# A feed-forward's gate and up products in one written order, their weights' low parts on VectorE, and the down weights loaded behind them without a wait

## The chip, the cores and the metric

One core of a Trainium2 chip runs the kernel. Its engines are TensorE (PE: matmuls), VectorE (DVE), ScalarE (ACT), GpSimd (POOL) and SyncE (SP), which issues all the DMAs. Each engine carries out its own instructions in the order in which they stand in its program and waits on semaphores for the others. The metric is the device time of one execution in microseconds (us); a run's median, lowest and highest are given. One execution was taken with a profiler; its span lies within its device time.

## The reference, cut to what matters

One layer of an encoder: 1024 positions, width 1024, in float32. A feed-forward, a mixer (two kinds of attention), and a second feed-forward, each between RMS norms and added to the input by half, whole, and half.

```python
def swiglu(x, w_gate, w_up, w_down):          # x 1024x1024, D_FF = 2816
    return (jax.nn.silu(x @ w_gate) * (x @ w_up)) @ w_down

f1 = swiglu(rms_norm(h, ffn1_pre_g), ffn1_w_gate, ffn1_w_up, ffn1_w_down)
h = h + 0.5 * rms_norm(f1, ffn1_post_g)
mix = hybrid_mixer(rms_norm(h, mix_pre_g), ...)
h = h + rms_norm(mix, mix_post_g)
f2 = swiglu(rms_norm(h, ffn2_pre_g), ffn2_w_gate, ffn2_w_up, ffn2_w_down)
h = h + 0.5 * rms_norm(f2, ffn2_post_g)
```

## The kernel before

*Precision.* A float32 operand is held as a high part, rounded to the matmul's type, and a low part, the rest. A product is three matmuls: high by high, high by low, low by high (`three`). To make the parts of a weight, ScalarE casts it to the high part (L521) and GpSimd subtracts that from the weight (L522); the helper is `split`.

*Fewer products.* `ffn` (L544) treats gate and up as 22 units (p, m): 11 pairs of 256 columns, p = 0 to 10, with m = 0 for gate and m = 1 for up. A unit is a 2x2 block product done with seven block products instead of eight (Strassen's scheme in Winograd's form). The seven left sides come from the raw weights: product 0, 1 and 3 are blocks of the raw tile; 4, 5, 6 and 2 are sums s1, s2, s3 and a second s2 made by VectorE (L593, L595, L597, L601). L601 overwrites the first s2, so it waits until the low part of product 5, which GpSimd makes from it, is done (`read2`). The right sides are seven combinations of X, made once (`X.ready`). A product is 12 matmuls of 512 columns (4 blocks of depth, three matmuls each, L641).

*PSUM.* Products 0 and 1 add up in one bank (tile b), 5 has a bank of its own, products 6 and 3 share one half of a pair of banks (tile s), 4 and 2 the other half. ScalarE copies product 0 (L667) to uu. VectorE then adds: uu + product 5 (L724), that + product 6 (L730), and from these the four blocks of the result: block 3 (L756), 2 (L768), 1 (L773). Product 3 writes on into the bank that L730 reads, so it has to wait for L730; product 2 waits for L756. Multiplications by the sigmoid (L686, L701) make the hidden values. For each pair VectorE and ScalarE then form seven combinations of the hidden values (L819 to L826) and their high and low parts (L795, L798); SyncE stores them to DRAM (hs_d, L799). The last pair is stored plain (hp_d).

*Down.* Pairs 0 to 9 make five groups of two pairs (g = 0 to 4), the last pair stands by itself. A group is again seven products; weights are loaded as rawd (four per group, L868), summed by VectorE (td, L887 to L897), split by ScalarE (wdb, L521) and GpSimd (L522); hidden pieces are loaded back as ha (L910); 168 matmuls a group (L1045); VectorE adds the results up (L994, L1084).

*What sets the order.* `Plan` (L126) is a small event-driven planner that runs while the program is built. Each piece of work is a Python generator; it yields events and tokens it waits for, and then work of an engine with a planned price (L262 to L278) and a rank. Whenever a planned engine is free, the waiting piece of the best rank is written into its program. The order that comes out is fixed; on the chip each engine follows it. Rooms for raw tiles and weight tiles are tokens (`raw_tok`, `w_tok`). In `gate_up` a unit is two processes, `head` (products 0 and 1) and `body` (5, 6, 4, 3, 2), so units may interleave as the planner's prices have it. `down_loads` begins only when the next to last pair is stored:

```python
        def down_loads():
            yield stored[NP - 2]
```

## Time and profile before

| | us |
|---|---|
| median of 3 runs | 2594.76 |
| lowest to highest | 2591.78 to 2595.79 |
| the profiled execution, device time | 2596.65 |
| its span | 2594.2 |
| TensorE busy | 2339.3 (90%) |
| VectorE busy | 1538.4 (59%) |
| GpSimd busy | 1225.7 (47%) |
| ScalarE busy | 1037.8 (40%) |

The profiled execution is 2.45 us longer than its span, and 1.9 us above the median. The mean granted clock of TensorE was 0.951 of full speed. The stretches of the span: the input's norm and the first combinations of X until about 56 us, gate and up of the first feed-forward until 511.9, the way into its down part until 550.2, that part until about 743, the mixer until about 1851, the second feed-forward's combinations until 1888.1, its gate and up until 2337.1, the way into down until 2370.0, and down and the last norm until the end. Matmuls are pipelined: a matmul's own duration (about 0.39 us) is longer than the distance to the next.

### The profile page before, as it was taken

How to read it: one execution, taken by the hardware profiler on the slowest of the kernel's cores; microseconds unless marked ns; L12 is line 12 of the kernel's file. 1: busy time of each engine (PE TensorE's matmuls, PEld its weight loads, DVE VectorE, ACT ScalarE, POOL GpSimd, SP SyncE). 2: the span in 40 equal slices, each digit the busy share in tenths (PEclk: the TensorE clock that was granted, in tenths of full speed). 3: DMA queues.
4: the chain of work that ended last, by engine and by line, in shares of the span. 5: the costliest groups of instructions: out<-in, count | busy, mean ns of one | idle time of the engine just before them, and what ended most of it. 6: DMA issues, size and time to landing. Idle time of an engine off the chain costs nothing. (4 is left out here: it accounts for less than half of the span.)

```text
span 2594.2 us, 31044 instructions
## 1 busy us (share of the span) xinstructions
PE 2339.3 (90%) x11096; PEld 1942.6 (75%) x11096; DVE 1538.4 (59%) x2359; ACT 1037.8 (40%) x1958; POOL 1225.7 (47%) x900
## 2 busy tenths in 40 slices
PE   6999999879988995999998998998799999997997
PEld 4777777658868984888887777876577777785885
DVE  8765667446574101676667677247856766564656
ACT  5333333231124232666655555444433333334111
POOL 4444455254466351665543223556345544535445
PEclk8999999989999997999999998998899999998998
DMA  4233344477633133212222222665324434357762
GB/s 140 104 129 139 110 163 158 162 278 253 231 100 122 40 102 107 57 53 84 81 65 81 86 86 78 231 211 195 138 70 152 160 118 151 113 215 274 258 234 97
DMA packets 198010, 364.86 MB, mean 141 GB/s; under 512 B 40608, under 2 KB 112800, under 8 KB 197344
## 3 DMA queue, kind: packets, MB, share of 16 engines
q1 hardware_dynamic: 197856, 362.89, 41.0%
q8 instruction: 87, 1.43, 0.2%
q14 instruction: 67, 0.55, 0.1%
HBM read 240.02 MB, written 122.81 MB: 140 GB/s over the span
## 5 line engine op out<-in xcount | busy, mean ns | idle before, releaser
L641 PE MATMUL s<-xh,wt 128*128 128x512 f32 x1408 | 468.6, 401 | 49.7 <-DVE uu L730 42.4
L522 POOL TENSOR_TENSOR wt<-s,wt 128x512 fp32r<-128x512 f32 x176 | 248.9, 1426 | 286.7 <-ACT wt L521 276.7
L641 PEld LDWEIGHTS s<-xh,wt 128*128 128x128 f32 x1408 | 271.5, 193 | 120.2 <-issue 52.0
L641 PE MATMUL b<-xh,wt 128*128 128x512 f32 x1056 | 344.4, 394 | 0.0
L522 POOL TENSOR_TENSOR wt<-raw,wt 128x512 fp32r<-128x512 f32 x132 | 197.4, 1505 | 201.1 <-ACT wt L521 130.3
L641 PE MATMUL s<-xl,wt 128*128 128x512 f32 x704 | 280.6, 399 | 0.0
L1045 PE MATMUL b<-wdb,ha 128*128 128x512 f32 x864 | 207.5, 396 | 35.1 <-ACT wdb L521 32.7
L641 PEld LDWEIGHTS b<-xh,wt 128*128 128x128 f32 x1056 | 201.5, 191 | 42.7 <-ACT xh L430 0.2
L1045 PEld LDWEIGHTS b<-wdb,ha 128*128 128x128 f32 x864 | 165.1, 192 | 72.2 <-ACT wdb L521 34.0
L641 PE MATMUL b<-xl,wt 128*128 128x512 f32 x528 | 207.4, 393 | 0.0
L1045 PE MATMUL s<-wdb,ha 128*128 128x512 f32 x816 | 194.2, 394 | 5.6 <-POOL wdb L522 3.6
L1045 PEld LDWEIGHTS s<-wdb,ha 128*128 128x128 f32 x816 | 155.0, 190 | 39.5 <-POOL wdb L522 4.4
L1870 POOL TENSOR_TENSOR p<-p,rd 128x1024 f32<-128x1024 f32 x64 | 120.7, 1894 | 101.1 <-DVE rd L1867 92.6
L1410 PE MATMUL b<-xh,wh 128*128 128x512 f32 x384 | 163.8, 427 | 0.0
L641 PEld LDWEIGHTS s<-xl,wt 128*128 128x128 f32 x704 | 135.9, 193 | 27.9
L1410 PE MATMUL b<-xl,wh 128*128 128x512 f32 x384 | 155.0, 404 | 0.0
L1410 PE MATMUL b<-xh,wl 128*128 128x512 f32 x384 | 154.2, 401 | 0.0
L522 POOL TENSOR_TENSOR wdb<-rawd,wdb 128x1024 fp32r<-128x1024 f32 x34 | 81.9, 2409 | 142.8 <-ACT wdb L521 139.7
L522 POOL TENSOR_TENSOR wdb<-td,wdb 128x1024 fp32r<-128x1024 f32 x40 | 100.1, 2503 | 92.9 <-ACT wdb L521 87.4
L522 POOL TENSOR_TENSOR wl<-raw,wh 128x512 fp32r<-128x512 f32 (+3 forms) x88 | 110.3, 1273 | 61.7 <-ACT wh L521 46.6
L601 DVE TENSOR_TENSOR s<-raw,s 128x512 f32<-128x512 f32 x44 | 72.9, 1658 | 101.3 <-POOL wt L522 101.3
L283 PE MATMUL s<-qkT,qkT 96*128 96x512 f32 x384 | 104.5, 406 | 21.9 <-ACT p L1860 21.9
(290 smaller groups left out, 5171.1 us busy)
## 6 DMA issues: line engine op xcount, KB each, us to landing
hs_d<-hl SPq DMA_DIRECT2D x140, 512.0 KB
ha<-hs_d SPq DMA_DIRECT2D x70, 1024.0 KB
raw<-in_ffn_w_gate_dram SPq DMA_DIRECT2D x44, 512.0 KB
raw<-in_ffn_w_up_dram SPq DMA_DIRECT2D x44, 512.0 KB
rawd<-in_ffn_w_down_dram SPq DMA_DIRECT2D x44, 512.0 KB
raw<-in_w_in_dram SPq DMA_DIRECT2D x28, 512.0 KB
h<-res SPq DMA_DIRECT2D x16, 512.0 KB
lg_d<-lg SPq DMA_DIRECT2D x32, 256.0 KB
```

The source lines that it names most:

```text
L283: T.matmul(o, l, r, start=(i == 0), stop=(i == n - 1))
L522: yield pool(n, lambda: G.tensor_sub(lo, src, hi))
L601: yield dve(512, lambda: V.tensor_sub(s2, L(0, 1), s2))
L641: T.matmul(out(), l, r, start=(first and k == 0 and n == 0), stop=(k == 3 and n == 2), skip_group_check=True,)
L1045: T.matmul(ps, l, r, start=(fresh and n == 0), stop=(n == 5), skip_group_check=True)
L1410: T.matmul(bs.ps, l, r, start=(part == 0 and n == 0), stop=(part == 7 and n == 2))
L1870: yield pool(S, lambda: G.tensor_tensor(bx.p, bx.p, bx.rd.broadcast_to([P, S]), op=ALU.mult))
```

## The change

The products of gate and up are written in one sequence `seq`: in the round of unit u come its product 0, then products 3 and 2 of the unit before, then its products 1, 5, 6 and 4. One process steps through it (`step`), in the place of `head` and `body`. The weights' parts follow the same sequence; the high part stays on ScalarE (L648), the low part is VectorE's (L649), where it was GpSimd's. A raw tile's two halves are waited for and freed each for itself. The processes that load and prepare the weights go on to the down weights with no wait for a store, and the down weights' rooms are the same tokens. A pair's token `gate_tok` is given back without a wait for its store. At the start of the second feed-forward three raw tiles may be loaded instead of two. The planner's price of a VectorE instruction rises by 0.05 us. The sums of a unit are now L615, L619, L622 and L626 (L593, L595, L597, L601 before), the PSUM additions L760, L771, L780, L793, L800 (L724, L730, L756, L768, L773), the products L675 (L641), the stores L829, the loads of down weights L900, of hidden pieces L942, the down sums L919, L922, L924, L929 (L887, L890, L892, L897), the additions of down L1028 (L994).

```diff
-        return ("dve", 0.1 + n * 0.00105, fn)
+        return ("dve", 0.15 + n * 0.00105, fn)
...
-        raw_tok, w_tok, hl_tok = Tokens(4 if room is None else 2), Tokens(6 if room is None else 2), Tokens(3)
+        raw_tok, w_tok, hl_tok = Tokens(4 if room is None else 3), Tokens(6 if room is None else 2), Tokens(3)
 
         def more():
             yield room
-            plan.release(raw_tok, 2)
+            plan.release(raw_tok, 1)
             plan.release(w_tok, 4)
 
         if room is not None:
             spawn(more(), 7)
         gate_tok = Tokens(2)
         units = [(p, m) for p in range(NP) for m in range(2)]
-        raws = {u: ([], Event(2)) for u in units}
+
+
+        seq = [(units[0], 0), (units[1], 0), (units[0], 1), (units[1], 1)]
+        for n, u in enumerate(units):
+            if n > 1:
+                seq.append((u, 0))
+            if n:
+                seq += [(units[n - 1], 3), (units[n - 1], 2)]
+            if n > 1:
+                seq.append((u, 1))
+            seq += [(u, 5), (u, 6), (u, 4)]
+        seq += [(units[-1], 3), (units[-1], 2)]
...
+            yield from down_loads()
...
+            def one(u, i):
+                bx, wx = sums[u], ws[*u, i]
+                ev = raws[u][1]
+                yield {0: ev[0], 1: ev[1], 2: bx.made[3], 3: ev[1], 4: bx.made[0], 5: bx.made[1], 6: bx.made[2]}[i]
+                L = bx.L
+                src = {
+                    0: lambda: L(0, 0), 1: lambda: L(0, 1), 2: lambda: bx.s2, 3: lambda: L(1, 1),
+                    4: lambda: bx.s1, 5: lambda: bx.s2, 6: lambda: bx.s3,
+                }[i]()
+                w = wx[0].w = slot([P, 2, 4, P], F32R, "wt")
+                yield act(512, lambda: A.copy(w[:, 0], src))
+                yield dve(512, lambda: V.tensor_sub(w[:, 1], src, w[:, 0]))
                 if i == 5:
-                    plan.set(read2)
-                plan.set(ev)
-                plan.set(used)
-
-            def free():
-                yield used
-                plan.release(raw_tok, 2)
-
-            spawn(combos(), 7)
-            spawn(free(), 7)
-            for i, src, after in (
-                (0, L(0, 0), None), (1, L(0, 1), None), (5, s2, made[1]), (6, s3, made[2]),
-                (4, s1, made[0]), (3, L(1, 1), None), (2, s2, made[3]),
-            ):
+                    plan.set(bx.read2)
+                if i in (0, 1, 3):
+                    plan.set(bx.used[0 if i == 0 else 1])
+                plan.set(wx[1])
...
+            for u, i in seq:
+                if u not in sums:
+                    begin(u)
+                if i == 1:
+                    spawn(sums[u].combos(), 7)
                 yield w_tok
-                ws[p, m, i][0].w = slot([P, 2, 4, P], F32R, "wt")
-                spawn(one(i, src, after), 7)
-
-        def prep():
-            for p, m in units:
-                yield from prep_unit(p, m)
+                spawn(one(u, i), 7)
+            yield from down_prep()
...
+        def step(u, i, ub):
...
+            elif i == 6:
+                yield S2
+                yield from product(u, 6, s_bank(0), True)
+
+                def second():
+                    yield ub.added[0]
+                    yield dve(512, lambda: V.tensor_add(u3(), ub.s[:, 0, :], u2()))
+                    plan.set(ub.added[1])
+
+                spawn(second(), 3)
...
+            elif i == 3:
+                yield ub.added[1]
+                yield from product(u, 3, s_bank(0), False)
...
+            else:
+                yield ub.read[3]
+                yield from product(u, 2, s_bank(1), False)
...
         def gate_up():
-            for u in units:
-                yield unit_tok
-                if u[1] == 0:
-                    yield gate_tok
-                ub = Box()
-                ub.m1 = Event()
-                spawn(head(u, ub), 8)
-                spawn(body(u, ub), 8)
-                if u[1] == 1:
-                    spawn(pair_done(u[0]), 5)
+            ubs = {}
+            for u, i in seq:
+                if u not in ubs:
+                    yield unit_tok
+                    if u[1] == 0:
+                        yield gate_tok
+                    ub = ubs[u] = Box()
+                    ub.m1 = Event()
+                    ub.added = [Event(), Event()]
+                    ub.read = [None, Event(), Event(), Event()]
+                    if u[1] == 1:
+                        spawn(pair_done(u[0]), 5)
+                yield from step(u, i, ubs[u])
+            plan.release(raw_tok, 2)
...
-            yield stored[p]
             plan.release(gate_tok)
...
-        rd_tok, t_tok = Tokens(6), Tokens(1)
+        rd_tok, t_tok = raw_tok, Tokens(1)
...
         def down_loads():
-            yield stored[NP - 2]
...
         def down_prep():
+            for _ in range(3):
+                yield w_tok
...
-        spawn(down_loads(), 8)
-        spawn(down_prep(), 8)
```

VectorE in the middle of the first gate and up, before, from the sum that waits for GpSimd (s is a weight sum or the PSUM tile, uu and c a unit's results, hs the hidden sums):

```order
L601 TENSOR_TENSOR s_267_1691<-raw_1604,s_267_1691 128x512 [waits Pool_49]
L730 TENSOR_TENSOR uu_1657<-s_1701,uu_1657 128x512 [waits PE_49]
L773 TENSOR_TENSOR uu_1518<-s_1572,uu_1518 128x512 [waits PE_49]
L701 TENSOR_TENSOR uu_1381<-uu_1518,uu_1381 128x512 [waits DVE_49]
L819 TENSOR_TENSOR hs_1755<-uu_1381 128x512 [waits DVE_49]
L821 TENSOR_TENSOR hs_277_1756<-sg_1450,uu_1381 128x512
L820 TENSOR_TENSOR hs_1755<-hs_1755,sg_1450 128x512 [waits DVE_49]
L756 TENSOR_TENSOR uu_1657<-s_1701,uu_1657 128x512 [waits PE_49]
```

After, VectorE from the addition of product 5 to that of product 6 (wt is a weight's high and low part, hl a hidden sum's):

```order
L760 TENSOR_TENSOR uu_1946<-b_2000,uu_1946 128x512 [waits DMAHW2_49,PE_49]
L615 TENSOR_TENSOR s_315_2014<-raw_1806,raw_1869 128x512 [waits DMAHW3_49]
L649 TENSOR_TENSOR wt_2013<-s_294_1865,wt_2013 128x512 [waits Activation_49]
L828 TENSOR_TENSOR hl_2046<-hs_1991,hl_2046 128x512 [waits Activation_49]
L828 TENSOR_TENSOR hl_2062<-hs_1991,hl_2062 128x512 [waits Activation_49]
L649 TENSOR_TENSOR wt_2039<-raw_1869,wt_2039 128x512 [waits DMAHW5_49]
L828 TENSOR_TENSOR hl_2081<-hs_309_1992,hl_2081 128x512 [waits Activation_49]
L619 TENSOR_TENSOR s_315_2014<-s_315_2014,raw_1806 128x512 [waits DVE_49]
L622 TENSOR_TENSOR s_316_2015<-raw_1806 128x512
L771 TENSOR_TENSOR uu_1946<-s_2026,uu_1946 128x512 [waits PE_49]
```

L626 waits for VectorE itself (it is not within these rows), and between the two additions stand eight others, two of them low parts of weights.

SyncE at the end of the first gate and up, before (hp_d are the last pair's stores, rawd the down weights, ha the hidden pieces):

```order
L799 DMA hp_d<-hl_3706 256x1x512 [waits DMAHW1_49,DVE_49]
L910 DMA ha_3716<-hs_d 128x2x1024 [waits DMAHW2_49,PE_49]
L799 DMA hp_d<-hl_3713 256x1x512 [waits DMAHW3_49,DVE_49]
L910 DMA ha_3719<-hs_d 128x2x1024 [waits DMAHW4_49,PE_49]
L868 DMA rawd_3721<-in_ffn_w_down_dram 128x2x512 [waits DMAHW5_49]
L868 DMA rawd_3723<-in_ffn_w_down_dram 128x2x512 [waits DMAHW6_49,Pool_49]
L868 DMA rawd_3728<-in_ffn_w_down_dram 128x2x512 [waits DMAHW7_49]
L868 DMA rawd_3754<-in_ffn_w_down_dram 128x2x512 [waits DMAHW0_49,Pool_49]
```

After, from the last raw weights of gate and up:

```order
L517 DMA raw_3349<-in_ffn_w_up_dram 128x4x256 [waits DMAHW2_49,PE_49]
L900 DMA rawd_3372<-in_ffn_w_down_dram 128x2x512 [waits DMAHW3_49]
L829 DMA hs_d<-hl_3463 128x1024 [waits DVE_49]
L900 DMA rawd_3468<-in_ffn_w_down_dram 128x2x512 [waits DMAHW5_49,PE_49]
L829 DMA hs_d<-hl_3466 128x1024 [waits DMAHW6_49,DVE_49]
```

The first two of the four loads of down weights now stand right behind the last raw weights, among the stores of the last but one pair (hs_d); the other two follow six rows further down, and the last pair's stores (hp_d) begin six rows behind those.

VectorE at the same place, before, from the last unit's results to the down weights' sums (td):

```order
L701 TENSOR_TENSOR uu_3421<-uu_3561,uu_3421 128x512 [waits DVE_49]
L768 TENSOR_TENSOR c_540_3680<-s_3614,uu_3561 128x512 [waits PE_49]
L701 TENSOR_TENSOR sg_3478<-c_540_3680,sg_3478 128x512 [waits DVE_49]
L773 TENSOR_TENSOR uu_3561<-s_3614,uu_3561 128x512
L701 TENSOR_TENSOR uu_3421<-uu_3561,uu_3421 128x512 [waits DVE_49,Activation_49]
L798 TENSOR_TENSOR hl_3703<-uu_3421,hl_3703 128x512 [waits Activation_49]
L798 TENSOR_TENSOR hl_3706<-sg_3478,hl_3706 128x512 [waits Activation_49]
L798 TENSOR_TENSOR hl_3713<-uu_3421,hl_3713 128x512 [waits DMAHW4_49,Activation_49]
L887 TENSOR_TENSOR td_3757<-rawd_3723,rawd_3721 128x1024 [waits DMAHW7_49,DMAHW6_49,DMAHW5_49]
L890 TENSOR_TENSOR td_3758<-rawd_3728,td_3757 128x1024 [waits DMAHW7_49,DMAHW0_49,DVE_49]
L892 TENSOR_TENSOR td_3759<-rawd_3728,rawd_3723 128x1024
L897 TENSOR_TENSOR td_3758<-rawd_3754,td_3758 128x1024 [waits DMAHW0_49,Pool_49]
```

After:

```order
L919 TENSOR_TENSOR td_3667<-rawd_3468,rawd_3372 128x1024 [waits DMAHW5_49,DMAHW3_49]
L800 TENSOR_TENSOR uu_3422<-s_3496,uu_3422 128x512 [waits DVE_49]
L697 TENSOR_TENSOR sg_3489<-b_3537,sg_3489 128x512 [waits PE_49]
L922 TENSOR_TENSOR td_3668<-rawd_3580,td_3667 128x1024 [waits DMAHW4_49,DMAHW2_49,DVE_49]
L924 TENSOR_TENSOR td_3669<-rawd_3580,rawd_3468 128x1024
L760 TENSOR_TENSOR uu_3572<-b_3627,uu_3572 128x512 [waits PE_49]
L929 TENSOR_TENSOR td_3668<-rawd_3625,td_3668 128x1024 [waits DMAHW5_49,Pool_49]
L771 TENSOR_TENSOR uu_3572<-s_3641,uu_3572 128x512 [waits DVE_49,PE_49]
L780 TENSOR_TENSOR uu_3572<-s_3641,uu_3572 128x512 [waits DVE_49,PE_49]
L712 TENSOR_TENSOR uu_3422<-uu_3572,uu_3422 128x512 [waits DVE_49]
```

The first group's sums td now stand ahead of the last unit's additions: L929, which waits for GpSimd, is in front of that unit's L771.

## Rows read from the trace of the kernel before

**Rows 1.** The page's busy line: engine, busy us, share of the span
```profile
PE 2339.3 (90%) x11096; PEld 1942.6 (75%) x11096; DVE 1538.4 (59%) x2359; ACT 1037.8 (40%) x1958; POOL 1225.7 (47%) x900
```

**Rows 2.** Table of stretches: us; busy PE, PEld, DVE, ACT, POOL; clock; DMA share; GB/s
```profile
14.00:56.30 42.30, 29.14 (x128) 21.61 (x129) 40.60 (x59) 26.67 (x50) 20.59 (x23) 0.84 0.33 105
56.30:511.90 455.60, 427.90 (x1818) 347.34 (x1816) 296.63 (x394) 153.95 (x283) 210.88 (x147) 0.97 0.38 137
511.90:550.20 38.30, 14.02 (x44) 10.20 (x44) 16.72 (x13) 11.67 (x15) 15.39 (x6) 0.69 0.62 226
550.20:720.00 169.80, 169.80 (x751) 140.60 (x750) 96.60 (x127) 38.96 (x45) 76.21 (x32) 1.00 0.70 245
1851.20:1888.10 36.90, 17.30 (x77) 12.57 (x77) 33.88 (x49) 17.54 (x31) 13.25 (x17) 0.65 0.48 163
1888.10:2337.10 449.00, 427.28 (x1830) 347.65 (x1828) 281.06 (x348) 154.56 (x284) 210.75 (x147) 0.98 0.39 141
2337.10:2370.00 32.90, 16.47 (x49) 11.88 (x49) 13.47 (x13) 11.78 (x15) 15.87 (x7) 0.69 0.62 235
```

**Rows 3.** TensorE's waits, gate-and-up of the first feed-forward: us, times, longest
```profile
PE s L641 <- DVE uu L730: 23.9, 11, 5.0
PE s L641 <- DVE sg L768: 3.0, 5, 1.4
PE s L641 <- DVE uu L756: 0.9, 1, 0.9
```

**Rows 4.** The same, gate-and-up of the second
```profile
PE s L641 <- DVE uu L730: 18.5, 9, 2.1
```

**Rows 5.** Timeline of VectorE, 308 to 320: start, us, instruction, [idle before]
```profile
314.71 1.74 DVE L601 TENSOR_TENSOR s<-raw,s 128x512 f32<-128x512 f32 x1 [5.84 <-POOL wt L522]
316.37 0.68 DVE L730 TENSOR_TENSOR uu<-s,uu 128x512 f32<-128x512 f32 x1
...
318.41 0.69 DVE L819 TENSOR_TENSOR hs<-uu 128x512 f32<-128x512 f32 x1
319.02 0.69 DVE L821 TENSOR_TENSOR hs<-sg,uu 128x512 f32<-128x512 f32 x1
```

**Rows 6.** Timeline of TensorE there
```profile
317.20 0.47 PE L641 MATMUL s<-xh,wt 128*128 128x512 f32 x1 [2.11 <-DVE uu L730]
```

**Rows 7.** Timeline of GpSimd there
```profile
313.38 2.52 POOL L522 TENSOR_TENSOR wt<-s,wt 128x512 fp32r<-128x512 f32 x2
```

**Rows 8.** Timeline of TensorE, first way into down
```profile
532.14 1.22 PE L1045 MATMUL b<-wdb,ha 128*128 128x512 f32 x2 [20.12 <-ACT wdb L521]
```

**Rows 9.** Timeline of ScalarE there
```profile
531.04 1.04 ACT L521 CAST wdb<-rawd 128x1024 fp32r<-128x1024 f32 x1 [14.43 <-DMA rawd<-in_ffn_w_down_dram]
```

**Rows 10.** Timeline of SyncE's queue there
```profile
500.04 17.46 SPq L799 DMA_DIRECT2D hp_d<-hl  x3
...
520.32 3.33 SPq L868 DMA_DIRECT2D rawd<-in_ffn_w_down_dram  x4
```

**Rows 11.** Timeline of TensorE, second way into down
```profile
2349.49 1.22 PE L1045 MATMUL b<-wdb,ha 128*128 128x512 f32 x2 [12.38 <-ACT wdb L521]
```

**Rows 12.** Groups of GpSimd, 150 to 480: shapes, count, busy us, mean ns
```profile
L522 POOL TENSOR_TENSOR wt<-s,wt 128x512 fp32r<-128x512 f32 x64 | 89.9, 1417 | 101.6 <-ACT wt L521 101.6
```

**Rows 13.** The same of VectorE
```profile
L601 DVE TENSOR_TENSOR s<-raw,s 128x512 f32<-128x512 f32 x16 | 28.1, 1755 | 38.7 <-POOL wt L522 38.7
...
L593 DVE TENSOR_TENSOR s<-raw,raw 128x512 f32<-128x512 f32 x16 | 15.3, 956 | 0.0
L756 DVE TENSOR_TENSOR uu<-s,uu 128x512 f32<-128x512 f32 x16 | 11.1, 691 | 29.5 <-PE s L641 29.4
```

**Rows 14.** Timeline of GpSimd, first way into down
```profile
532.16 2.35 POOL L522 TENSOR_TENSOR wdb<-rawd,wdb 128x1024 fp32r<-128x1024 f32 x1 [37.02 <-ACT wdb L521]
```

**Rows 15.** Timeline of VectorE there
```profile
535.63 3.28 DVE L890 TENSOR_TENSOR td<-rawd,td 128x1024 f32<-128x1024 f32 x1
538.83 1.21 DVE L892 TENSOR_TENSOR td<-rawd,rawd 128x1024 f32<-128x1024 f32 x1
```

More of the change, by code (lines that the diff above doesn't have):

```diff
@@ L555, in ffn @@
         units = [(p, m) for p in range(NP) for m in range(2)]
-        raws = {u: ([], Event(2)) for u in units}
+        seq = [(units[0], 0), (units[1], 0), (units[0], 1), (units[1], 1)]
[8 more added lines that the diff above has]
+        seq += [(units[-1], 3), (units[-1], 2)]
+        raws = {u: ([None, None], [Event(), Event()]) for u in units}
         ws = {(*u, i): (Box(), Event()) for u in units for i in range(7)}
@@ L633, in product @@
         def product(u, i, out, first):
+            yield X.ready[i]
+            yield ws[*u, i][1]
             def write():
@@ L648, in product @@
                 plan.release(big_tok)
-        def head(u, ub):
-            p, m = u
-            for i in (0, 1):
-                yield X.ready[i]
-                yield ws[*u, i][1]
-            yield B1
-            bx = Box()
-            def out():
-                if not hasattr(bx, "ps"):
-                    bx.ps = bank()
-                return bx.ps
-            yield from product(u, 0, out, True)
-            def cp():
-                ub.uu = slot([P, 2, 512], name="uu")
-                A.copy(ub.uu[:, 0, :], bx.ps)
-            yield act(512, cp)
-            plan.set(ub.m1)
-            yield from product(u, 1, out, False)
-            spawn(c11(u, ub, bx), 4)
         def c11(u, ub, bx):
             p, m = u
+            bx.ps = ub.b1
             if m == 0:
@@ L702, in block @@
             plan.set(hid[p][n])
-        def body(u, ub):
+        def step(u, i, ub):
             p, m = u
-            yield X.ready[5]
-            yield ws[*u, 5][1]
-            yield B1
-            bb, bs = Box(), Box()
-            ub.read = [None, Event(), Event(), Event()]
-            def out_b():
-                if not hasattr(bb, "ps"):
-                    bb.ps = bank()
-                return bb.ps
-            yield from product(u, 5, out_b, True)
-            added = [Event(), Event()]
@@ L776, in body, with b_bank, out, s_bank @@
-            yield ub.read[1]
-            plan.release(S2)
-            plan.release(unit_tok)
+            def b_bank(key):
+                def out():
+                    if not hasattr(ub, key):
+                        setattr(ub, key, bank())
+                    return getattr(ub, key)
+                return out
+            def s_bank(n):
+                def out():
+                    if not hasattr(ub, "s"):
+                        ub.s = two_banks()
+                    return ub.s[:, n, :]
+                return out
```

156 lines of the change are left out of this document (83 added, 73 removed).

## The prediction

> **What bounds the kernel now.** I read the page's busy line first [rows 1]: TensorE is busy for 90% of the span, so only what stops TensorE costs time. Then the table of stretches [rows 2]. The fourth stretch, the first feed-forward's down part, is TensorE at its limit: 751 matmuls in 169.80 us, all of them busy, granted clock 1.00, so 0.2261 us for a matmul of 512 columns. With that price each other stretch splits into work and loss:
> - gate-and-up of the first feed-forward: 455.6 us for 1818 matmuls; 1818 × 0.2261 = 411.1, loss 44.5 us;
> - the way from there into down: 38.3 us for 44 matmuls (9.9), loss 28.4;
> - gate-and-up of the second: 449.0 us for 1830 (413.8), loss 35.2;
> - its way into down: 32.9 us for 49 (11.1), loss 21.8.
> Together 130 us that TensorE does not need. The change touches these four stretches; the mixer between the two feed-forwards and the ends stay as they are.
>
> The list of waits says who holds TensorE inside gate-and-up [rows 3, 4]: nearly always the second PSUM addition on VectorE, L730 (23.9 us in 11 waits, 18.5 in 9). But L730 itself is short. The timeline of one such place shows the chain [rows 5 to 7]: VectorE stands at L601 for 5.84 us because GpSimd's low part of product 5 is not there; GpSimd does its two pieces from 313.38 in 2.52 us; L601 then takes 1.74 us, L730 (316.37) follows, and TensorE resumes at 317.20 after 2.11 us idle. So the bound is VectorE's program order: an addition that was ready stands behind an instruction that waits for the slow GpSimd. The three waits of the first feed-forward add up to 27.8 of its 44.5 us [rows 3]; the rest is clock: the stretch ran at 0.97 [rows 2], where the down stretch without idle ran at 1.00.
>
> The ways into down are something else [rows 8 to 10]: TensorE idles 20.12 us for ScalarE's first down-weight cast, ScalarE waits 14.43 us for the load, and the load stands in SyncE's queue at 520.32 behind stores of the last pair, which wait from 500.04 for 17.46 us. In the second feed-forward the first stall is 12.38 us [rows 11].
>
> **The change, part by part.**
> (1) *Low parts on VectorE.* 308 subtractions of 128x512 leave GpSimd (1.42 us each [rows 12]), 14 for each of 22 pairs, and join VectorE. There an operation without company takes 0.69 us (L756 [rows 13]), and back to back they start 0.61 us apart (318.41, 319.02 [rows 5]). VectorE now holds 47 instructions a pair: between 47 × 0.61 = 28.7 and 47 × 0.69 = 32.4 us. A pair's 168 matmuls need 168 × 0.2261 = 38.0 us. So VectorE goes to 75 to 85% and is not the bound. The wait at L601 (now L626) is gone: its releaser is an instruction of VectorE itself, a few rows ahead. And with GpSimd idle in this part, the sums of two SBUF operands fall from 0.96 and 1.76 us (L593, L601) to about 0.69 [rows 13]. The other end of the price: if they stayed at 0.96, 47 × 0.956 = 44.9 us a pair (rival D).
> (2) *Fixed order.* A unit's products 3 and 2 come two places into the next unit's round. So from the end of product 5 to product 3, which needs L771, TensorE now does product 6, product 4 and the next unit's product 0: 3 × 2.71 us (12 matmuls each), 8.1 us, where it was two products and 5.4. In this time VectorE does L760 (0.68), then by the order eight others, 8 × 0.61 = 4.9, then L771 (0.68), 6.3 in all: 1.8 us are left in this round, more in the others by the same count. No wait by this count, but not every round will be clean: a late cast of ScalarE takes up 1.8 us soon. I leave 6 us of loss in each feed-forward (bounds 0 and 25, some half of what is lost now or more): gain 38.5 and 29.
> (3) *Down loads follow at once.* The first four loads of down weights stand amid gate-and-up in SyncE's queue, ahead of the stores of the last pair. So the 20.12 and 12.38 us go. What is late next: (a) VectorE's L929 (before L897) waits for GpSimd's low part of a down weight, the fourth in GpSimd's row at 2.35 us [rows 14], and the second addition L771 that the last unit's product 3 needs stands behind it. Counted from the end of that unit's product 5: the sum L922, beside GpSimd from −2.0, ends at 1.2 (3.28 us), its cast (1.04 us [rows 9]) at 2.2, GpSimd's turn from 3.8 to between 6.2 and 6.9, L929 1.21 to 3.28 us (alone or beside GpSimd [rows 15]), L771 0.68: 8.1 to 10.9, where TensorE is ready at 6.3. A stall of 1.8 to 4.6, I take 3. (b) The second group's down weights stand in SyncE's queue behind six loads of hidden pieces, each waiting for a product of the first group. Its first cast (1.04 us) stands behind a copy that waits for that group's last product, and after the cast comes 2.35 us of GpSimd: about 3 us of stall. (c) The sums of the second group stand behind additions of its first product: about 3 us more. With a lower clock behind each stop, 10 us in all (bounds 4 and 20). Gain 28.4 − 10 = 18 and 21.8 − 10 = 12.
> (4) *Starts.* From 14 to 56 us VectorE is full: busy 40.60 of 42.30 [rows 2], and 14 more low parts stand in front of the last pieces of X, 14 × 0.61 = 8.5 us later. Against it: the sums lose GpSimd's company (for two units' sums 2 × (3 × 0.27 + 1.07) = 3.8 us, by [rows 13]), and 25 more products' matmuls stand ahead of the last transposition on TensorE, 25 × 0.2261 = 5.7 us done early. Between −5 and +4; I take −1. In the second feed-forward 24 more early matmuls (5.4 us) run where TensorE has gaps, while five or six more VectorE instructions stand in a stretch where VectorE is busy 33.88 of 36.90 us [rows 2]: 0 to +4, I take +2.
> (5) The planner's price for VectorE and the third token of raw weights only shape the order; the order is read off as it is, so they cost nothing by themselves. The token `gate_tok` no longer waits for stores: nothing shown waits there, 0.
>
> Sum: −38.5 − 29 − 18 − 12 − 1 + 2 = −96.5. The profiled execution took 2596.65 us (span 2594.2 and 2.45 outside), which is 1.9 above the median of the three, 2594.76. So 2500.2 by the profiled one, **2498** by the median.
>
> One rule of the Trainium skill speaks against part (1). "Perfetto Trace Analysis", section "Optimizing Scalar/DVE Operations", says that VectorE and GpSimd share an SBUF read port, so that shifting operations between the two might not help. By that rule alone gate-and-up would keep its loss and the time would be rival C's. The rows disagree as far as they go: the same 128x512 difference takes 1.42 us on GpSimd and 0.69 on VectorE, and the sharing is seen as the 0.96 and 1.76 us of sums that go beside GpSimd. The move ends the sharing in this part.
>
> **The rivals.**
> A. *All is recovered.* No round waits and the ways into down keep under 4 us of stall: 2594.8 − 130 + 1 = 2466, up to 2480. For it: the down stretch shows that the same matmuls run with no idle at all. Against it: (3a) is in the order plainly.
> B. *The stall into down only moves.* SyncE now feeds hidden pieces, weights and stores in one queue; if the first product waits for its hidden piece, or the second group waits for all of its loads, each way keeps its loss: 2594.8 − 38.5 − 29 + 1 = 2528 (2515 to 2540). For it: (3b); DMA moved 226 GB/s in that stretch already [rows 2]. Against it: four loads at least are long done.
> C. *VectorE's order still holds TensorE.* 14 low parts a pair stand in the same queue as the additions, each waiting for a cast of ScalarE, which waits for TensorE to give a weight slot back. If every round loses 2 us, as it does now, gate-and-up gains nothing and only part (3) is left: 2594.8 − 30 + 1 = 2566 (2545 to 2580). For it: only about 1.8 us of slack. Against it: lookahead of five to six products of 2.71 us on the low parts.
> D. *VectorE becomes the bound, slower than before.* The price is that of sums that go beside other work, 0.956 us, for all 47: 44.9 us a pair, 494 us a feed-forward, 38 and 45 us more than now; less 30 for the ways in: 2594.8 + 83 − 30 = 2648. It decides from the point where a pair takes over 41.4 + 1.4 us (455.6/11 and a share of the 30), so 0.91 us an instruction. Against it: no instruction alone took that, and GpSimd is silent there.
> E. *The change doesn't do what it says*, the waits at L730 being due to the additions' own late matmuls: same time within 0.2%, about 5 us, which is what a measurement can tell. The order already shows the moved rows.
>
> **Chances.** Forecast (2480 to 2515) 0.57; A 0.12; B 0.14; C 0.09; D 0.05; E 0.03. Faster by over 0.2%: 0.57 + 0.12 + 0.14 + 0.09 = 0.92, less 0.01 for a loss I have not seen, 0.91; same 0.03; slower 0.06. The range takes the forecast, B, most of A and the lower part of C: 2468 to 2550.
>
> **What would show it.** Right: in gate-and-up of the new profile VectorE 75 to 85% busy, no instruction of GpSimd, low parts at 0.69 us, TensorE's waits for VectorE under 6 us in each, granted clock 0.99 or 1.00, the stretch near 418 us. In the way into down: loads of down weights before the last stores, ScalarE's first cast long before TensorE needs it, and stops of some 3 us at the last unit's product 3 and at the second group. Wrong: sums of 0.9 us with GpSimd silent (D); waits of 2 us at L771 in each round (C); one stop of over 10 us into down (B); X's last piece more than 4 us later than now.

## The result, and the profile after

The changed kernel takes 2506.68 us (median of 4 runs, 2503.58 to 2510.06) where the kernel before took 2595.28 beside it (4 runs, 2591.78 to 2600.2): ratio 0.9658, 95% interval 0.9637 to 0.9679. It is 88.6 us faster; 97 were forecast, and 2506.7 lies in the forecast's own stretch (2480 to 2515). The profiled executions differ by 91.0 us of span (2594.2 to 2503.2).

The table of stretches, to be laid beside [rows 2] (us; busy us and instructions of PE, PEld, DVE, ACT, POOL; clock; DMA share; GB/s). The rows are: start, gate-and-up, the way into down, the down part; then start, gate-and-up and the way into down of the second feed-forward:

```profile
14.00:60.10 46.10, 32.92 (x147) 24.43 (x148) 43.38 (x70) 28.80 (x55) 10.64 (x15) 0.85 0.35 112
60.10:463.00 402.90, 402.90 (x1777) 332.96 (x1776) 320.09 (x534) 158.20 (x283) 9.13 (x4) 1.00 0.43 151
463.00:545.00 82.00, 69.39 (x283) 55.24 (x282) 39.92 (x43) 25.32 (x36) 35.87 (x13) 0.94 0.72 272
545.00:676.90 131.90, 131.90 (x584) 109.21 (x583) 76.62 (x112) 21.11 (x20) 54.93 (x23) 1.00 0.63 217
1806.10:1846.00 39.90, 22.23 (x96) 16.24 (x97) 36.35 (x56) 21.02 (x38) 8.96 (x14) 0.66 0.43 148
1846.00:2245.00 399.00, 399.00 (x1761) 329.88 (x1760) 305.49 (x482) 156.62 (x278) 8.37 (x3) 1.00 0.43 152
2245.00:2330.00 85.00, 72.98 (x300) 58.20 (x299) 41.14 (x44) 26.17 (x37) 39.49 (x16) 0.94 0.73 277
```

Gate-and-up is now what the down part was before: TensorE busy in all of its 402.90 us, clock 1.00. By the prediction's price of a matmul 1777 × 0.2261 = 401.8, so 1.1 us of loss where there were 44.5; in the second, 399.0 − 398.2 = 0.8 where there were 35.2. The list of TensorE's waits is empty in both. The way into down still loses 82.0 − 283 × 0.2261 = 18.0 us, and 85.0 − 300 × 0.2261 = 17.2 in the second.

VectorE in the middle of gate-and-up, 150 to 440 us (groups as in [rows 13]):

```profile
L649 DVE TENSOR_TENSOR wt<-s,wt 128x512 fp32r<-128x512 f32 x60 | 39.4, 686 | 21.4 <-ACT wt L648 21.4
L771 DVE TENSOR_TENSOR uu<-s,uu 128x512 f32<-128x512 f32 x15 | 10.3, 687 | 33.3 <-PE s L675 33.3
L626 DVE TENSOR_TENSOR s<-raw,s 128x512 f32<-128x512 f32 x15 | 10.2, 683 | 0.0
L615 DVE TENSOR_TENSOR s<-raw,raw 128x512 f32<-128x512 f32 x15 | 10.2, 681 | 0.0
```

The sum that waited for GpSimd has no idle time before it and takes 0.683 us for 1.755; the sum L615 takes 0.681 for 0.956. L771 now waits for TensorE, and no longer TensorE for it. In that window VectorE was busy 219.5 of 290 us, 76%, and GpSimd carried out nothing:

```profile
150.00:440.00 290.00, 290.00 (x1281) 240.01 (x1280) 219.50 (x355) 113.30 (x205) 0.00 (x0) 1.00 0.41 146
```

What is left of the way into down is a list of five waits in the first feed-forward (us, times, longest), and the same five in the second within 0.6 us:

```profile
PE s L675 <- DVE uu L771: 6.1, 1, 6.1
PE s L1079 <- POOL wdb L522: 2.4, 1, 2.4
PE s L1079 <- DVE bacc L1028: 2.2, 1, 2.2
PE b L1079 <- POOL wdb L522: 1.7, 1, 1.7
PE s L1079 <- ACT wdb L521: 0.3, 1, 0.3
```

The first is the one that the order showed. The timelines there of VectorE, GpSimd and TensorE:

```profile
457.20 2.93 DVE L922 TENSOR_TENSOR td<-rawd,td 128x1024 f32<-128x1024 f32 x1
460.06 3.43 DVE L924 TENSOR_TENSOR td<-rawd,rawd 128x1024 f32<-128x1024 f32 x1
463.41 0.68 DVE L760 TENSOR_TENSOR uu<-b,uu 128x512 f32<-128x512 f32 x1
465.74 3.34 DVE L929 TENSOR_TENSOR td<-rawd,td 128x1024 f32<-128x1024 f32 x1 [1.65 <-POOL wdb L522]
469.00 0.68 DVE L771 TENSOR_TENSOR uu<-s,uu 128x512 f32<-128x512 f32 x1
```

```profile
462.37 3.34 POOL L522 TENSOR_TENSOR wdb<-td,wdb 128x1024 fp32r<-128x1024 f32 x1
465.66 2.34 POOL L522 TENSOR_TENSOR wdb<-rawd,wdb 128x1024 fp32r<-128x1024 f32 x1
467.96 3.33 POOL L522 TENSOR_TENSOR wdb<-td,wdb 128x1024 fp32r<-128x1024 f32 x1
```

```profile
469.83 0.76 PE L675 MATMUL s<-xh,wt 128*128 128x512 f32 x1 [6.10 <-DVE uu L771]
470.39 0.63 PE L675 MATMUL s<-xl,wt 128*128 128x512 f32 x1
470.81 1.05 PE L675 MATMUL s<-xh,wt 128*128 128x512 f32 x2
```

VectorE and GpSimd hold each other up here: L924 takes 3.43 us, where such a sum alone takes 1.21 [rows 15], and GpSimd's piece for which L929 waits takes 3.34, where one alone takes 2.38 (the last section has the rule). L929 starts 1.65 us after L760's end, when that piece is done, takes 3.34, and L771 follows at 469.00; TensorE, which goes on at 469.83, had waited since 463.7. Behind the stop its matmuls start 0.42 to 0.43 us apart, not 0.2261: mostly the lower of the clock's two levels (granted clock 0.57 from 470.0 to 476.2). The other stops belong to the second group, whose down weights SyncE issues late, behind seven loads of hidden pieces:

```profile
486.30 8.25 SPq L942 DMA_DIRECT2D ha<-hs_d  x7
494.65 1.68 SPq L900 DMA_DIRECT2D rawd<-in_ffn_w_down_dram  x1
499.12 0.36 SPq L942 DMA_DIRECT2D ha<-hs_d  x1
499.54 7.22 SPq L900 DMA_DIRECT2D rawd<-in_ffn_w_down_dram  x3
```

The mixer, from its first product to its last, before and after:

```profile
768.10:1851.20 1083.10, 989.61 (x5344) 850.28 (x5344) 583.97 (x1138) 552.73 (x1137) 517.84 (x424) 0.95 0.34 105
```

```profile
714.60:1806.10 1091.50, 994.40 (x5368) 854.84 (x5368) 591.84 (x1147) 553.34 (x1138) 511.17 (x419) 0.95 0.34 105
```

It is 8.4 us longer. 24 more of its TensorE instructions are gate-and-up matmuls of the second feed-forward done early (5368 − 5344; 24 × 0.2261 = 5.4 us); 3.0 us are left.

### The profile page after: what moved, and what is told of

Its sections match the earlier page's. It is cut to its first block, busy times and chain, and to the rows that moved or that the text cites. A ratio compares the mean times of both kernels' runs of the same rounds, so it can differ in the third digit from the quotient of the medians.

```text
span 2503.2 us, 30709 instructions
## 1 busy us (share of the span) xinstructions
PE 2311.5 (92%) x11096; PEld 1930.7 (77%) x11096; DVE 1595.3 (64%) x2667; ACT 1042.4 (42%) x1958; POOL 797.8 (32%) x592
## 5 line engine op out<-in xcount | busy, mean ns | idle before, releaser
L675 PE MATMUL s<-xh,wt 128*128 128x512 f32 x1408 | 452.9, 393 | 13.2 <-DVE uu L771 12.2
L522 POOL TENSOR_TENSOR wdb<-rawd,wdb 128x1024 fp32r<-128x1024 f32 x34 | 87.4, 2574 | 958.7 <-ACT wdb L521 958.7
L675 PE MATMUL b<-xh,wt 128*128 128x512 f32 x1056 | 343.4, 392 | 1.9 <-ACT uu L744 0.7
L675 PEld LDWEIGHTS s<-xh,wt 128*128 128x128 f32 x1408 | 266.3, 189 | 72.4 <-issue 13.3
L675 PE MATMUL s<-xl,wt 128*128 128x512 f32 x704 | 275.7, 392 | 0.0
L675 PEld LDWEIGHTS b<-xh,wt 128*128 128x128 f32 x1056 | 199.2, 189 | 44.5 <-DVE wt L649 1.1
L675 PE MATMUL b<-xl,wt 128*128 128x512 f32 x528 | 206.5, 391 | 0.6 <-DVE xl L431 0.6
L649 DVE TENSOR_TENSOR wt<-s,wt 128x512 fp32r<-128x512 f32 x176 | 120.1, 710 | 54.1 <-ACT wt L648 54.1
L675 PEld LDWEIGHTS s<-xl,wt 128*128 128x128 f32 x704 | 133.3, 189 | 26.9
L522 POOL TENSOR_TENSOR wdb<-td,wdb 128x1024 fp32r<-128x1024 f32 x40 | 107.6, 2694 | 71.4 <-ACT wdb L521 71.4
L426 PE MATMUL b<-cst,p 128*128 128x128 f32 x768 | 107.9, 282 | 23.8 <-DVE ptd L431 14.7
L426 PEld LDWEIGHTS b<-cst,p 128*128 128x128 f32 x768 | 91.5, 145 | 40.9 <-DVE ptd L431 17.3
```

The costliest lines, as they stand in the source:

```text
L426: T.transpose(b[:rows, i * P : (i + 1) * P], src(i), ident)
L522: yield pool(n, lambda: G.tensor_sub(lo, src, hi))
L649: yield dve(512, lambda: V.tensor_sub(w[:, 1], src, w[:, 0]))
L675: T.matmul(out(), l, r, start=(first and k == 0 and n == 0), stop=(k == 3 and n == 2), skip_group_check=True,)
```

## The experiments

There are twelve runs: eleven new kernels, and the changed one again. Ratios are to the kernel before, timed beside each.

**The planner's price.** The changed kernel with the new price inside the feed-forwards only:

```diff
     def dve(n, fn):
-        return ("dve", 0.15 + n * 0.00105, fn)
+        return ("dve", 0.1 + n * 0.00105, fn)
...
     def ffn(X, wg, wu, wd, post, hs, hp, started=None, room=None):
+        def dve(n, fn):
+            return ("dve", 0.15 + n * 0.00105, fn)
```

> The changed kernel, but the planner's new VectorE price (0.15) holds only inside the feed-forwards; elsewhere it is 0.1 as before. In the changed kernel the mixer took 1091.5 us from its first product to its last, 1083.1 before. Theory (the price reorders the mixer's instructions and that costs the time): the mixer is back at 1083 +-2 us and the median is about 2498. Rival (the mixer is slower because it starts 54 us earlier, or by how memory lies after the other feed-forward): the mixer stays at 1091 and the median at 2506.7 +-2.

Measured 2509.11 us, ratio 0.9662 (0.9647 to 0.9677). The theory fell: the mixer's instructions are again nearly in the old order, and it takes 1094.1 us with the same 5368 instructions. It runs as before for 990 us (5001 instructions of TensorE in 990.2 us, in 990.0 before) and loses its 11 us at the end, where the first products of the second feed-forward stand between its own (369 instructions in 103.9 us, 345 in 93.1 before). The reverse, the kernel before with nothing but the new price:

```diff
-        return ("dve", 0.1 + n * 0.00105, fn)
+        return ("dve", 0.15 + n * 0.00105, fn)
```

> The kernel before, with nothing but the planner's VectorE price at 0.15. Theory (the price alone makes the mixer's new order): the mixer takes 1090 +-3 us instead of 1083; gate-and-up may move by some us, since its order changes too, but its waits for the addition behind GpSimd stay at 15 to 30 us in each feed-forward, and both ways into down keep 35 us and more: median 2595 to 2610. Rival (the price is a part of what freed gate-and-up): the waits there fall below 10 us and the median falls under 2580.

Measured 2588.6 us, ratio 0.9962 (0.9947 to 0.9977): a little faster, outside the range expected. The mixer took 1082.0 us in its new order. Gate-and-up kept its stops at L730 (23.8 and 18.4 us); the first stop into down fell from 20.1 to 13.3 us. So the price explains neither the mixer nor the gain. Inside the feed-forwards it was not tried by itself in the changed kernel.

**The low parts alone.** The kernel before with this and nothing else:

```diff
-                yield from split(src, bx.w[:, 0], bx.w[:, 1], 512)
+                yield act(512, lambda: A.copy(bx.w[:, 0], src))
+                yield dve(512, lambda: V.tensor_sub(bx.w[:, 1], src, bx.w[:, 0]))
```

> The kernel before with nothing but the low parts of gate and up weights moved to VectorE; the planner's own order, its prices and the late down loads stay. Theory (the move alone frees gate-and-up): TensorE's stops there fall from 28 and 22 us to under 8 in each feed-forward, the stretches run at a clock of 0.99 or more, the ways into down still stop 10 to 20 us, and the median is 60 to 75 us below the kernel before (2520 to 2540). Rival (14 more instructions a pair in the planner's loose order hold the additions as GpSimd did): stops of over 15 us in each feed-forward remain and the median falls by less than 35 us.

Measured 2519.93 us, ratio 0.9705 (0.9686 to 0.9724). As the theory said, at the lower edge of its range. Its waits of over 0.5 us from 60 us on, to the end of the first way into down:

```profile
PE b L1046 <- ACT wdb L521: 14.2, 1, 14.2
PE s L1046 <- POOL wdb L522: 2.6, 1, 2.6
PE b L1046 <- POOL wdb L522: 1.2, 1, 1.2
PE s L642 <- DVE uu L731: 0.9, 1, 0.9
PE s L642 <- DVE uu L757: 0.9, 1, 0.9
```

The second feed-forward has the same waits within 0.1 us. So gate-and-up has 1.8 us of stops without any fixed order, and the late down load costs 14.2 us.

**The order without the low parts.** The changed kernel with them back on GpSimd:

```diff
-                yield dve(512, lambda: V.tensor_sub(w[:, 1], src, w[:, 0]))
+                yield pool(512, lambda: G.tensor_sub(w[:, 1], src, w[:, 0]))
```

> The changed kernel with the low parts of gate and up weights back on GpSimd; the fixed order and the early down loads stay. Theory (the waits for the slow low part behind L626 are the cause, whatever the order): L626 waits for GpSimd again, TensorE's stops at L771 come back in most rounds, 10 to 25 us in each feed-forward, sums of two SBUF operands take 0.95 us again, and the median is 1 to 2% above the changed kernel's (2530 to 2555). Rival (the order alone gives the addition its room, 8.1 us instead of 5.4): gate-and-up keeps under 5 us of stops in each feed-forward and the median stays within 10 us of the changed kernel's.

Measured 2647.63 us, ratio 1.0195 (1.0173 to 1.0217): slower than the kernel before, and above the theory's 2530 to 2555. Its gate-and-up of the first feed-forward, waits and stretch:

```profile
PE s L675 <- DVE uu L780: 52.8, 12, 5.8
PE s L675 <- DVE uu L771: 5.3, 2, 3.9
```

```profile
60.00:550.00 490.00, 431.97 (x1777) 350.79 (x1776) 316.76 (x391) 160.86 (x288) 229.34 (x152) 0.93 0.37 128
```

One stop of mostly 4.3 us a pair, at L780 and not at L771 as the theory had it, and a clock of 0.93. The rows of one of them, VectorE's and TensorE's:

```profile
296.11 1.74 DVE L626 TENSOR_TENSOR s<-raw,s 128x512 f32<-128x512 f32 x1 [1.18 <-POOL wt L649]
297.77 0.68 DVE L771 TENSOR_TENSOR uu<-s,uu 128x512 f32<-128x512 f32 x1
298.37 0.67 DVE L828 TENSOR_TENSOR hl<-hs,hl 128x512 fp32r<-128x512 f32 x1
298.97 0.68 DVE L780 TENSOR_TENSOR uu<-s,uu 128x512 f32<-128x512 f32 x1
```

```profile
299.80 0.47 PE L675 MATMUL s<-xh,wt 128*128 128x512 f32 x1 [4.32 <-DVE uu L780]
```

The two additions stand behind the sum that waits for GpSimd, as L730 did before; this fixed order leaves them there.

**The one wait put back.**

```diff
         def down_loads():
+            yield stored[NP - 2]
```

> The changed kernel, but the loads of down weights again begin only when the next to last pair is stored (the one wait put back). Theory (the early loads are what removed the 20.1 and 12.4 us stops): stops of 8 to 20 us come back at the first down products of each feed-forward, GpSimd's and ScalarE's first down piece comes after the last unit's products, and the median rises by 15 to 40 us to 2522 to 2546; gate-and-up stays without stops. Rival (the fixed order alone would have opened the way, since the last pair's stores come earlier): the median rises by less than 6 us.

Measured 2521.62 us, ratio 0.9709 (0.9695 to 0.9724): 12 to 13 us slower than the changed kernel, a little under the theory's range. Gate-and-up has no stop. Each way into down has two, of 18.2 and 4.9 us and of 17.8 and 4.9, together 23.1 and 22.7, in place of five of 12.6 and 12.1.

**The stop at L771.** First by the planner alone: the sum waits for an event that the last unit's second addition sets.

```diff
...
                 yield read5
+                if g == 0:
+                    yield last_added
```

> The changed kernel; the first group's last sum of down weights (L929, the one that waits for GpSimd's low part) is ordered behind the last unit's second PSUM addition. Theory (TensorE's 6.1 us stop at the last unit's product 3, once in each feed-forward, is this instruction standing in front of the addition): both stops fall below 1 us, and the median falls by 10 to 14 us to about 2494, the lower clock after the stop included. Rival (the addition waits for something else, or the saved time is lost at the next stop, where GpSimd's low parts are late): the stops stay at 6 us, or later stops of the first group grow by 4 to 6 us each, and the median is 2503 to 2508.

Measured 2510.34 us, ratio 0.9664 (0.965 to 0.9678), the 6.1 us stops unchanged. This says nothing for the rival: on VectorE the sum still stood in front of L771. The planner's event did not move it (that the framework under the planner orders once more is likely, but not shown). An edge given to the framework itself did:

```diff
...
-                yield dve(1024, lambda: V.tensor_sub(tb.t2, R(1, 0), tb.t2))
+                if g == 0:
+                    yield last_added
+
+                def last_sum():
+                    s = V.tensor_sub(tb.t2, R(1, 0), tb.t2)
+                    if g == 0:
+                        tc.add_manual_dep(s.ins, ubs[units[-1]].second.ins.name, ...)
+
+                yield dve(1024, last_sum)
```

> The changed kernel; the first group's last sum of down weights (L929) is bound behind the last unit's second PSUM addition (L771) by an edge of order, so that the two rows really change places on VectorE. Theory (the 6.1 us stop at the last unit's product 3 is that sum standing in front): the stop at L771 falls below 0.5 us, a smaller one of 1 to 3 us may stand at the next addition (L780), which now comes behind the sum; the median falls by 5 to 11 us against the changed kernel's (ratio to before 0.962 to 0.964). Rival (the time is lost again at the first group's later products): the first stop goes, later ones grow by as much, ratio 0.965 to 0.967.

Measured 2500.75 us, ratio 0.963 (0.9613 to 0.9647). VectorE's rows now, right behind L760:

```profile
465.09 0.69 DVE L772 TENSOR_TENSOR uu<-s,uu 128x512 f32<-128x512 f32 x1
466.65 3.40 DVE L940 TENSOR_TENSOR td<-rawd,td 128x1024 f32<-128x1024 f32 x1 [0.87 <-POOL wdb L522]
469.98 0.68 DVE L785 TENSOR_TENSOR uu<-s,uu 128x512 f32<-128x512 f32 x1
```

L772 is the old L771, L940 the sum L929. The stop of 6.1 us became stops of 1.3 and 1.0; the later stops grew by 0.3 and 1.1 us in the two feed-forwards, where two executions of the changed kernel differ by up to 2.3. The theory held: this one row cost some 4 us in each (0.963 for 0.9663 is 8.6 us).

**The later stops.** The same sum on GpSimd, and the further raw rooms given back at the last unit's first product, two edits together:

```diff
-                yield dve(1024, lambda: V.tensor_sub(tb.t2, R(1, 0), tb.t2))
+                yield (pool(...) if g == 0 else dve(...))
...
                 yield from step(u, i, ubs[u])
-            plan.release(raw_tok, 2)
+                if (u, i) == (units[-1], 0):
+                    plan.release(raw_tok, 2)
```

> The changed kernel with that sum (first group only) made by GpSimd, behind the low part that it waits for, and with the two further raw rooms given back at the last unit's product 0 instead of after the last product, so that two of the second group's down weights are loaded ahead of the first group's hidden pieces. Theory (the first stop is VectorE's order, the later ones, 6.5 and 5.9 us, the late weights of the second group): stops in each way into down fall from 12.6 and 12.0 us to 2 to 6 us and the median falls by 12 to 22 us against the changed kernel's (ratio 0.957 to 0.961). Rival (the later stops are GpSimd's speed, 2.3 to 3.4 us for each of its pieces, to which another piece is added): they stay or grow by 2 to 4 us each, and the ratio is 0.962 to 0.966.

Measured 2493.45 us, ratio 0.9607 (0.9589 to 0.9624). Stops of 7.4 us are left (4.8, 1.6, 1.0) for 12.6; the 4.8 is a cast of the second group, whose third load still stood behind hidden pieces. The time is within the theory's range, the stops are above its 2 to 6 us; which edit gave how much was not tried.

**Whether the fixed order is needed.** Three kernels and a repeat of the changed one beside the first two:

> The changed kernel once more, unchanged, beside the next two, to have its time on the same chip. It was 0.9658 of the kernel before, so 0.964 to 0.968 is expected.

Measured 2508.75 us, ratio 0.9663 (0.9647 to 0.9679).

The kernel before with the low parts on VectorE (the edit above) and

```diff
         def down_loads():
-            yield stored[NP - 2]
+            yield stored[NP - 3]
```

> The kernel before with the low parts of gate and up weights on VectorE, and the loads of down weights begun one stored pair earlier (the third to last pair's store instead of the next to last); no fixed order, no shared rooms, the old price. Theory (the low parts and the early loads are the whole gain, the fixed order has no part in it): TensorE's stops in gate-and-up stay under 3 us in each feed-forward, the first stop of 14 us into down shrinks to 3 to 8 us, and the ratio to the kernel before is 0.961 to 0.967, like the changed kernel's. Rival (the fixed order is what lets the way into down be closed): stops of 10 us or more stay there, or move to the last unit's additions, and the ratio stays at 0.969 or above.

Measured 2478.16 us, ratio 0.9554 (0.9541 to 0.9567): below the theory's range, and 30.6 us under the changed kernel beside it. Its only stop from 60 to 560 us is one of 3.1 (L731, behind the same sum of down weights), and the second feed-forward has the same one. Then with that sum on GpSimd for the first group, as above:

> That kernel, with the first group's last sum of down weights made by GpSimd instead of VectorE. Theory (the sum stands in front of the last unit's second addition here as in the changed kernel and costs some 6 us in each feed-forward): the stop at the last unit's product 3 goes, and the time is 8 to 13 us below that kernel's, ratio 0.957 to 0.962. Rival (GpSimd's extra piece makes the first group's later products late): less than 4 us below it.

Measured 2469.91 us, ratio 0.9515 (0.9502 to 0.9528), the best of all: 38.8 us under the changed kernel, and 8.3 under the last, at the lower end of the theory. No stop is left in either way into down; the stretch that holds it in the first feed-forward:

```profile
430.00:545.00 115.00, 115.00 (x508) 94.74 (x507) 82.80 (x95) 45.85 (x66) 56.21 (x21) 1.00 0.83 301
```

At last the fixed order with the other kernel's loads, so that the order comes apart from rooms and chaining:

```diff
-        rd_tok, t_tok = raw_tok, Tokens(1)
+        rd_tok, t_tok = Tokens(6), Tokens(1)
...
         def down_loads():
+            yield stored[NP - 3]
...
-            yield from down_loads()
...
-            yield from down_prep()
...
-            plan.release(raw_tok, 2)
...
-            for _ in range(3):
-                yield w_tok
...
+        spawn(down_loads(), 8)
+        spawn(down_prep(), 8)
```

> The changed kernel (fixed order, low parts on VectorE, new price) with the down weights' loads as in the kernel of the old order that was 0.9554 of the kernel before: six rooms of their own and a start at the third to last pair's store; the shared rooms and the chaining behind the gate and up loads go. Theory (the second group's late weights, which come from the shared rooms, cost the changed kernel its 17 us into each down part, and the fixed order costs little): the stops in each way fall from 12 us to under 5, its loss from 17 to under 8 us, and the ratio is 0.956 to 0.961. Rival (the fixed order itself is what is slow): the ways keep 10 us of stops or gate-and-up gets new ones, and the ratio is 0.963 to 0.968.

Measured 2477.75 us, ratio 0.9541 (0.9528 to 0.9554): the time of the old order, below the theory's range. Its gate-and-up and its way into down:

```profile
60.10:463.00 402.90, 400.64 (x1766) 330.56 (x1765) 318.86 (x535) 157.66 (x284) 5.20 (x2) 1.00 0.44 155
463.00:545.00 82.00, 81.55 (x360) 67.22 (x359) 48.94 (x56) 30.52 (x41) 43.48 (x18) 1.00 0.90 317
```

In the 82.0 us in which the changed kernel did 283 matmuls this one did 360: the loss there is 82.0 − 81.4 = 0.6 us, and 402.9 − 1766 × 0.2261 = 3.6 in the stretch before, 1.1 in the changed kernel. SyncE's rows show what moved. The changed kernel's first four loads of down weights, then this one's first five:

```profile
412.98 0.84 SPq L900 DMA_DIRECT2D rawd<-in_ffn_w_down_dram  x1
431.57 0.38 SPq L900 DMA_DIRECT2D rawd<-in_ffn_w_down_dram  x1
446.75 1.93 SPq L900 DMA_DIRECT2D rawd<-in_ffn_w_down_dram  x2
```

```profile
413.83 17.54 SPq L898 DMA_DIRECT2D rawd<-in_ffn_w_down_dram  x5
```

The first load goes out at 413 us in both. The last two of the first group went out at 447, here at 417 and 420; the second group's came from 494.65 on, here from 431. So what the changed kernel lost into down, the stop at L771 included, came from the loads' start, their rooms and their chaining, which this run changes together, and not from the order of the products.

## Why the prediction was right, and where it was not

*Part (1), low parts on VectorE: right, and nearly the whole of it.* By itself it gave 77 us where the whole change gives 89 (2596.9 to 2519.9); the rest is about what the wait of `down_loads` costs when it is put back, 12 to 13. VectorE was 76% busy where 75 to 85% was said, a low part took 0.686 us where 0.69 was said. Rival D is out by these two numbers. Rival C is out by the empty list of waits. The Trainium skill ("Perfetto Trace Analysis", section "Optimizing Scalar/DVE Operations") says that a move between these two engines might not help; here it did. What was moved stood in a chain, and beside GpSimd the same sum took 2.6 times as long (L601 1.755 us, L626 0.683).

*Part (2), 6 us left in each: too much.* 1.1 and 0.8 us are left. The gain is 43.4 and 34.4 for the 38.5 and 29 forecast, 10.3 us together. And the reason given, that the order's 8.1 us give the addition room, is not the cause: without the order the stops are 1.8 us, with the order and GpSimd's low parts they are 58.1 in the first feed-forward.

*Part (3), 10 us left in each: the term that was sized wrong.* 18.0 and 17.2 us were left; the gain is 10.4 and 4.6 for 18 and 12, 15 us less. The places were right: L771 behind L929, and two more at the second group, from its late loads. (a) was 6.1 and not 3. Counted as there from the end of the last unit's product 5, at 457.4 us by the trace: L922 ended at 2.7 and not at 1.2, since it began at −0.2 and not at −2.0; GpSimd's piece ran from 5.0 to 8.3 and not from 3.8 to 6.9 at most, behind L922's late end and L924; L771 ended at 12.3 and not at 10.9 at most. TensorE was ready at 6.3, as counted. (b) and (c), 3 us each, were 2.4, 1.7 and 2.2 us, 6.5 with the cast. The rest, 18.0 − 12.6 = 5.4 us, is the clock behind the stops, 0.94 over the stretch, for which I had left 1. Rival B's sign, one stop of over 10 us, did not come, but of the 50.2 us that the ways lost before, 35.2 stayed, which puts rival A out too. And against B I had said that four loads are long done: the last two of them went out at 447 us, 16 before TensorE stopped.

*Part (4), starts: right in size, the second one not in place.* X's last transposition ends 5.1 us later (55.0 to 60.1), with 25 more matmuls done by then (26 to 51, 5.7 us): net −0.6 for −1. In the second, the mixer and the start together took 1083.1 + 36.9 = 1120.0 us and take 1091.5 + 39.9 = 1131.4, with 43 more matmuls done (9.7 us): 1.7 us longer, for +2. But this is the mixer, which I had put at nothing and which is 3.0 us longer than its early matmuls explain; VectorE's full stretch, where I had expected the +2, loses 39.9 − 96 × 0.2261 = 18.2 us where it lost 36.9 − 77 × 0.2261 = 19.5.

*Sum.* 0.6 + 43.4 + 34.4 + 10.4 + 4.6 − 1.7 = 91.7 us by these rows, 91.0 by the spans. That the forecast of 97 is near is in part luck: an error of 10 us and one of 15 lay on opposite sides.

*Part (5), price and tokens at nothing.* Outside the feed-forwards the price costs nothing (0.9662 without it, 0.9663 with it); inside them it was not tried by itself, and in the kernel before the whole of it gave 0.4%. The shared rooms, of which the prediction says nothing, cost together with the chaining some 31 us (0.9541 and 0.9663): the first group's loads came late and the second's later. That the fixed order costs nothing against the planner's was shown (0.9541 and 0.9554). Why the mixer is longer stays open in part: in every kernel here with the fixed order and its third raw tile it holds 24 more early matmuls (5.4 us) and takes 1089 to 1095 us, in every one without 1080 to 1083.

## What to carry to other kernels

Where a fast engine stands at an instruction that waits for a slow one, look for what is queued behind it: here a 0.69 us operation moved to the fast engine freed the additions behind it, and with both engines' queues apart the order hardly mattered. Where an engine has two prices for one operation, alone and beside a neighbour, find out which of the two starts first: the other one pays. Prefetches for the next stage want rooms and a queue place of their own: chained behind the present stage's loads and sharing its rooms, they came earlier here than behind a store, but the second group too late, and a kernel with rooms of their own was 1.2% faster.

## What the runs showed of the hardware

A VectorE sum of two SBUF operands and a GpSimd piece (the low part of a down weight) do not run side by side: the one that starts second waits for the other's end. Alone, a 128x1024 one takes 1.21 us on VectorE [rows 15], and on GpSimd, with VectorE idle:

```profile
518.69 2.38 POOL L522 TENSOR_TENSOR wdb<-rawd,wdb 128x1024 fp32r<-128x1024 f32 x1
```

In the rows of the stop above, GpSimd's piece at 465.66 starts first and takes its 2.34 us; L929 starts 0.08 us later, takes 3.34 and ends 1.08 after it. The next piece, at 467.96, starts before L929's end, takes 3.33 and ends 2.21 after it. So it is wherever the two meet in the changed kernel's down parts: 12 sums end 1.08 us after a piece that started first, 20 pieces 2.2 to 2.3 us after such a sum. The 2.35 us of [rows 14], which the prediction took for the price, is such a first one; VectorE's sum paid for it:

```profile
532.33 3.27 DVE L887 TENSOR_TENSOR td<-rawd,rawd 128x1024 f32<-128x1024 f32 x1 [14.83 <-issue]
```

An addition with one operand in PSUM is not held up: L760 takes 0.68 us at 463.41, in the middle of the piece that began at 462.37. With a GpSimd that is silent, the 128x512 sums took 0.68 to 0.69 us throughout.

A way into down whose stops add up to 12.6 us loses 18.0: the granted clock was 0.94 over that stretch (0.57 from 470.0 to 476.2, behind the longest stop), and 1.00 in the kernel whose stops there were 0.5 us.
